# One fused diffusion block: rotation factors held per token block, and the group norm of a quarter of the tokens inside the scan's last window

## The chip, the cores and the metric

The kernel runs on one core of a Trainium2 chip. A core has TensorE (PE; its weight loads are shown apart as PEld), VectorE (DVE), ScalarE (ACT), GpSimd (POOL), and SyncE (SP), which here issues all transfers; each engine takes its own queue in order. The metric is device microseconds of one launch, the median of three runs. All arithmetic is fp32: a matmul operand is split into a high and a low part, and each product is three matmuls (high x high, low x high, high x low).

## The reference

One layer over 2048 latent tokens of width 1024 and 256 context tokens:

```
h  = modulate(rmsnorm(x)); q, k, v, rw, gl = split(h @ w_in)
q, k = apply_rope(q), apply_rope(k)                  # x*cos + swapped(x)*sin
ya = latent_window_attention(q, k, v, kc, vc, sink)  # |i-j| <= 128, and the context
y  = wkv7_scan(forward) + wkv7_scan(reverse)         # RWKV-7, 8 heads of 64
yn = (y - mu) * rsqrt(var + eps)                     # group norm, per token and head
yr = (yn * lnx_w + lnx_b + bonus) * (sigmoid(hg) @ gate_g2)
x  = x + gate1 * ((ga*(ya @ w_branch_attn) + gr*(yr @ w_branch_rwkv)) @ w_out)
x  = x + gate2 * (relu(modulate(rmsnorm(x)) @ w_up)**2 @ w_down)
```

## The kernel before

**Stages.** Projection and preparation (0 to about 1085 us) go through the tokens in blocks of up to 512 and, for each block, through groups of 128 columns of `w_in`. Each of the five groups that are rotated (four of q, one of k) calls `rope()` (L239): it loads the factors `cs` (cosine and sine, 128 x 2 x n) into the one buffer that `cs` has, copies the swapped quarters of the PSUM tile to `sw` on ACT (L245), multiplies by the sine on POOL (L246) and by the cosine on DVE (L247), and adds on POOL (L248).

The scan (about 1085 to 2401 us) has 36 steps in 9 windows of four; each step advances both directions by 64 tokens, and its chain of small matmuls (`ch`, L535, with `g` copied to SBUF by ACT at L687) is serial from step to step. Beside the chain run two generators, a piece at a time: `attend()` (attention) and `fill()` (first the merge gates, then `branch()`, L970: `ya @ w_branch_attn`, PSUM tile `gt`, results to `ma_d`). Also one piece of `ada2` (the later modulation rows, `mods`) runs per step. The first half of the steps writes y to `y_d`; the second half loads what the other direction left (`yo`), adds and stores.

The merge (about 2401 to 2797 us) takes token blocks of 512 in the order 1, 0, 2, 3. `rwkv_out(tb)` (L1141) loads `yT` from `y_d`, transposes it (`mt`, L1149), takes mean and variance per head on DVE, the power on POOL (L1160), scales on POOL (L1161), transposes back (L1170), applies `lnx_w` and `lnx_b` on ACT, adds the bonus `btile` on POOL (L1175), multiplies by the gate (matmul L1177, DVE L1178) and splits into `yr_h`, `yr_l`. Then come the `mb` matmuls (branch R, L1240 to L1242), the sum with `ma_d`, the `mm` matmuls with `w_out` (L1258 to L1260), the residual and `second_norm`. For the first block, `merge_weights()` (L1202) is called after the `mb` matmuls: it multiplies `w_out` by `gate1` (DVE L1223, tile `x1t`) and splits it into `wo_h`, `wo_l` (L1224, L1225), for use by all four blocks. The MLP (to the end) reads the second norm's output back from `h2_d` into `h2h`, `h2l`, with `up_h`, `up_l` for its first matmuls `fu`.

**What sets the order.** The program is written in one order; a scheduler then interleaves the instructions on each engine by its own simulated timeline, and the resulting order is fixed at build time. SBUF addresses come from pools, opened and closed as stacks; a tile that overlaps an earlier pool's tile waits until the last reader of that one is done.

## Time and profile before

| | |
|---|---|
| time, median of 3 runs | 4223.32 us (4220.43 to 4228.75) |
| the profiled execution | 4228.56 us, span 4226.8 us, mean granted clock 0.932 |
| PE busy | 3865.3 us, 91% |
| DVE, ACT, POOL busy | 2171.9, 1359.5, 1349.6 us |
| HBM traffic | 529.95 MB, 125 GB/s over the span |

Busy time is a sum over stages with different limits. In the MLP PE has no gap; ahead of it the gaps differ by stage. The granted clock is a share of full speed (1.0 is 2.4 GHz, 0.5 is 1.2 GHz), so a stretch at 0.5 counts as busy and still does half the work.

### The profile page before, as it was taken

Reading aid. Unit: us, or ns where it says so; the run is one execution under the profiler, and the core shown is the slowest. Engines: PE = TensorE matmul, PEld = TensorE weight load, DVE = VectorE, ACT = ScalarE, POOL = GpSimd, SP = SyncE. Lnnn points to the kernel's source line nnn. Section 1 sums busy time; section 2 is a strip of 40 time slices with the busy share of each in tenths; the row PEclk is TensorE's granted clock in tenths of the full one; section 3 lists DMA queues with packets and bytes.
Section 4 is the critical chain, followed back from the end, with each engine's and each line's share of the span. In section 5 each row is a group of like instructions: output and inputs, shape, how many; then the busy total and the mean of one; then the engine's idle time right before and its main releaser. Section 6 shows DMA issues by size and latency. Waiting matters only on the chain.

```text
span 4226.8 us, 67796 instructions
## 1 busy us (share of the span) xinstructions
PE 3865.3 (91%) x26788; PEld 3148.4 (74%) x26788; DVE 2171.9 (51%) x3794; ACT 1359.5 (32%) x2476; POOL 1349.6 (32%) x1104
## 2 busy tenths in 40 slices
PE   7989978897899989888898779989999999999999
PEld 5778868785677767766676658768888888888887
DVE  3355277767576366556566364444443345444334
ACT  2353444554343333322322233331212213112121
POOL 3353555554221110000000174533433334443231
PEclk8999979897999989797897889999999999999999
DMA  6665566666544445343442545542211214211111
GB/s 236 202 195 158 161 183 188 188 185 184 164 138 138 125 131 148 106 132 96 131 139 83 158 150 179 176 154 65 70 50 40 60 41 130 69 60 60 40 55 45
DMA packets 617587, 529.95 MB, mean 125 GB/s; under 512 B 156212, under 2 KB 536340, under 8 KB 616244
## 3 DMA queue, kind: packets, MB, share of 16 engines
q1 hardware_dynamic: 617268, 525.60, 41.6%
q8 instruction: 211, 3.46, 0.3%
q14 instruction: 108, 0.88, 0.1%
HBM read 381.09 MB, written 144.38 MB: 124 GB/s over the span
## 4 chain that ended last, share of the span: by engine, by line
PE 58%; DVE 6%; DMA 4%; issue 2%; POOL 2%; SPq 1%; ACT 1%; POOLq 0%; DVEq 0%; ACTq 0%
PE fd L1343 5%; PE fd L1344 5%; PE fd L1345 5%; PE fu L235 5%; PE fu L236 5%; PE fu L237 5%; PE ch L535 5%; PE gt L947 3%; PE ops L883 3%; PE gb L535 2%; DVE au L582 1%; PE sc L835 1%; PE mm L1260 1%; PE mm L1258 1%; PE mm L1259 1%
## 5 line engine op out<-in xcount | busy, mean ns | idle before, releaser
L235 PE MATMUL acc<-hh,w_hi 128*128 128x384 f32 (+6 forms) x1304 | 457.4, 353 | 41.6 <-ACT hh L211 18.9
L237 PE MATMUL acc<-hh,w_lo 128*128 128x384 f32 (+6 forms) x1304 | 455.8, 351 | 10.3 <-POOL w_lo L229 10.3
L236 PE MATMUL acc<-hl,w_hi 128*128 128x384 f32 (+6 forms) x1304 | 456.5, 351 | 4.8 <-POOL hl L212 4.8
L1349 DVE TENSOR_TENSOR acc<-fd,acc 128x512 f32<-128x512 f32 x480 | 322.3, 686 | 249.1 <-PE fd L1345 246.8
L235 PE MATMUL fu<-h2h,up_h 128*128 128x512 f32 x1024 | 403.4, 394 | 5.8 <-ACT rl L1330 5.8
L1343 PE MATMUL fd<-dn_h,g_h 128*128 128x512 f32 x1024 | 399.8, 390 | 3.5 <-DVE acc L1347 3.5
L236 PE MATMUL fu<-h2l,up_h 128*128 128x512 f32 x1024 | 402.6, 393 | 0.0
L237 PE MATMUL fu<-h2h,up_l 128*128 128x512 f32 x1024 | 402.0, 393 | 0.0
L1333 DVE TENSOR_TENSOR g_l<-rl,g_h 128x512 fp32r<-128x512 f32 x128 | 150.0, 1173 | 487.4 <-POOL rl L1332 487.4
L1344 PE MATMUL fd<-dn_l,g_h 128*128 128x512 f32 x1024 | 399.7, 390 | 0.0
L1345 PE MATMUL fd<-dn_h,g_l 128*128 128x512 f32 x1024 | 398.3, 390 | 0.0
L235 PEld LDWEIGHTS acc<-hh,w_hi 128*128 128x128 f32 (+2 forms) x1304 | 256.1, 197 | 67.1 <-ACT hh L211 21.8
L1332 POOL TENSOR_TENSOR rl<-rl 128x512 f32<-128x512 f32 x128 | 149.9, 1171 | 469.2 <-ACT g_h L1331 469.1
L229 POOL TENSOR_TENSOR w_lo<-w_raw,w_hi 128x1024 fp32r<-128x1024 f32 (+1 forms) x92 | 232.7, 2532 | 205.9 <-ACT w_hi L228 185.7
L1330 ACT ACTIVATE rl<-fu 128x512 f32<-128x512 f32 x128 | 76.2, 597 | 654.1 <-PE fu L237 644.9
L237 PEld LDWEIGHTS acc<-hh,w_lo 128*128 128x128 f32 (+2 forms) x1304 | 255.7, 196 | 31.4 <-POOL w_lo L229 12.5
L236 PEld LDWEIGHTS acc<-hl,w_hi 128*128 128x128 f32 (+2 forms) x1304 | 256.0, 196 | 25.1 <-POOL hl L212 6.0
L1287 POOL TENSOR_TENSOR dn_l<-raw,dn_h 128x1024 fp32r<-128x1024 f32 x64 | 155.6, 2450 | 275.1 <-ACT dn_h L1286 275.1
L845 DVE TENSOR_REDUCE mm<-sc 128x1 f32<-128x256 f32 (+1 forms) x256 | 119.0, 477 | 237.9 <-PE sc L837 152.2
L235 PEld LDWEIGHTS fu<-h2h,up_h 128*128 128x128 f32 x1024 | 193.1, 189 | 49.3 <-ACT rl L1330 6.0
L1343 PEld LDWEIGHTS fd<-dn_h,g_h 128*128 128x128 f32 x1024 | 192.9, 188 | 44.9 <-DVE acc L1347 4.0
L237 PEld LDWEIGHTS fu<-h2h,up_l 128*128 128x128 f32 x1024 | 192.7, 188 | 43.5
(305 smaller groups left out, 8292.3 us busy)
## 6 DMA issues: line engine op xcount, KB each, us to landing
w_raw<-in_w_in SPq DMA_DIRECT2D x74, 512.0 KB
raw<-in_w_mlp_up SPq DMA_DIRECT2D x64, 512.0 KB
raw<-in_w_mlp_down SPq DMA_DIRECT2D x64, 512.0 KB
bk_d<-bk SPq DMA_DIRECT2D x36, 512.0 KB
w<-v_d SPq DMA_DIRECT2D x144, 128.0 KB
gw_raw<-in_w_in SPq DMA_DIRECT2D x32, 512.0 KB
ada_w<-in_w_ada SPq DMA_DIRECT2D x32, 512.0 KB
gt<-g_d SPq DMA_DIRECT2D x64, 256.0 KB
```

The lines of the kernel that those rows point to most:

```text
L229: pool.tensor_tensor(out=lo[:, :, :m], in0=raw[:, :, :m], in1=hi[:, :, :m].bitcast(F32), op=ALU.subtract)
L235: pe.matmul(ps[:m, :n], wh[:, k, :m], hh[:, k, :], start=(k == 0), stop=False)
L236: pe.matmul(ps[:m, :n], wh[:, k, :m], hl[:, k, :], start=False, stop=False)
L237: pe.matmul(ps[:m, :n], wl[:, k, :m], hh[:, k, :], start=False, stop=(k == KC - 1))
L535: return self.link(nc.tensor.matmul(*a, **k))
L1287: eng.tensor_tensor(out=lo, in0=raw, in1=hi.bitcast(F32), op=ALU.subtract)
L1332: pool.tensor_tensor(out=rl, in0=rl, in1=rl, op=ALU.mult)
L1333: dve.tensor_tensor(out=glo[:, j], in0=rl, in1=gh[:, j].bitcast(F32), op=ALU.subtract)
L1343: pe.matmul(ps, lh, dn[j][0][:, cs], start=(j == 0), stop=False)
L1344: pe.matmul(ps, lh, dn[j][1][:, cs], start=False, stop=False)
L1345: pe.matmul(ps, ll, dn[j][0][:, cs], start=False, stop=(j == FG - 1))
L1349: dve.tensor_tensor(out=acc[:, cs], in0=ps, in1=acc[:, cs], op=ALU.add)
```

## The change

Four things. `rope()` keeps its factor tile for all groups of one token block and pass, so that 25 loads become 5; `sw` has one buffer where it had two, and `sg` of the preparation shares the buffer of `ksq`. A new generator `early()` does the whole of `rwkv_out` but the split for tokens 512 to 1023 inside the scan's last window, in four iterations of 128 tokens, with attention's PSUM banks and the SBUF buffers of four tags of the scan's pool; it stores to `yw_d`, and `rwkv_out(1)` becomes four loads and splits. The `ada2` pieces run one and two per step in turn, so that they end by step 24. `merge_weights()` is called ahead of the block loop, its gate2 part after the loop over `w_out`, and `wo_h`, `wo_l` become one tile per 128 rows, half of them in a new pool `mv` that is opened last, while `mp` (the tiles of `rwkv_out`) is opened first.

```diff
+    EB0, EBN = 512, 512
+    yw_d = dram.tile([NP, P, EBN], F32, name="yw_d")
...
+    rope_of = {}
+
     def rope(ps, t0, n, dst):
         l0 = t0 - CTX
-        cs = epool.tile([P, 2, 512], F32, name="cs", bufs=1)
-        sp.dma_start(out=cs[:, :, :n], in_=io["rope"][:, :, l0:l0 + n])
-        sw = epool.tile([P, 512], F32, name="sw")
+        if t0 not in rope_of:
+            m = 512 if n > 384 or n == 256 else 384
+            rope_of[t0] = epool.tile([P, 2, m], F32, name=f"cs{m}", bufs=1)
+            sp.dma_start(out=rope_of[t0][:, :, :n], in_=io["rope"][:, :, l0:l0 + n])
+        cs = rope_of[t0]
+        sw = epool.tile([P, 512], F32, name="sw", bufs=1)
...
-            sg = prep.tile([96, W], F32, name="sg")
+            sg = prep.tile([96, W], F32, name="sg", tag="ksq", bufs=1)
...
+    def early():
+        wk = [ip.tile([P, 4, NP, P], F32, name="yw0", tag="ga", bufs=1), ip.tile([P, 4, NP, P], F32, name="yw1", tag="st")]
+        aw = ip.tile([P, 1024], F32, name="g2e", tag="au", bufs=1)
+        sg = ip.tile([P, 2, P], F32, name="sge", tag="itmp", bufs=1)
+        g2 = aw[0:96, 0:512]
+        sp.dma_start(out=g2, in_=io["gate_g2"])
+        def load(i):
+            t0 = EB0 + i * P
+            for j in range(P // C):
+                sp.dma_start(out=wk[i % 2][:, 0, :, j * C:(j + 1) * C], in_=y_d[t0 // C + j])
+            sp.dma_start(out=sg[0:96, i % 2], in_=sg_d[:, t0:t0 + P])
+            sp.dma_start(out=wk[i % 2][:, 3], in_=bon_d[:, :, t0:t0 + P].rearrange("a p t -> p a t"))
+        load(0)
+        for i in range(EBN // P):
+            yT, yc, yw, bt = (wk[i % 2][:, j] for j in range(4))
+            s1 = aw[:, 512 + i % 2 * 2 * H:512 + (i % 2 + 1) * 2 * H].rearrange("p (b h) -> p b h", h=H)
+            if i + 1 < EBN // P:
+                load(i + 1)
+            ps = bank(atp, "ey", "at")
+            for p in range(NP):
+                pe.transpose(ps[:, p * P:(p + 1) * P], yT[:, p], ident)
+            y3 = ps.rearrange("p (h c) -> p h c", c=C)
+            dve.tensor_reduce(out=s1[:, 0], in_=y3, axis=AX.X, op=ALU.add)
+            dve.tensor_scalar(out=s1[:, 0], in0=s1[:, 0], scalar1=-1.0 / C, scalar2=None, op0=ALU.mult)
+            ycf = yc.rearrange("p a b -> p (a b)")
+            y3c = ycf.rearrange("p (h c) -> p h c", c=C)
+            dve.tensor_tensor(out=y3c, in0=y3, in1=s1[:, 0].unsqueeze(2).broadcast_to([P, H, C]), op=ALU.add)
+            act.activation(yw, yc, AF.Square)
+            dve.tensor_reduce(out=s1[:, 1], in_=yw.rearrange("p a b -> p (a b)").rearrange("p (h c) -> p h c", c=C),
+                              axis=AX.X, op=ALU.add)
+            pool.tensor_scalar(out=s1[:, 1], in0=s1[:, 1], scalar1=1.0 / C, scalar2=1e-5 * C, op0=ALU.mult, op1=ALU.add)
+            pool.tensor_tensor(out=s1[:, 1], in0=s1[:, 1], in1=expo[:, :H], op=ALU.pow)
+            pool.tensor_tensor(out=y3c, in0=y3c, in1=s1[:, 1].unsqueeze(2).broadcast_to([P, H, C]), op=ALU.mult)
+            yield
+            ps = bank(atp, "eb", "at")
+            for p in range(NP):
+                pe.transpose(ps[:, p * P:(p + 1) * P], yc[:, p], ident)
+            for p in range(NP):
+                act.activation(yw[:, p], ps[:, p * P:(p + 1) * P], AF.Identity, scale=col(O_LW + p), bias=col(O_LB + p))
+            pool.tensor_tensor(out=yw, in0=yw, in1=bt, op=ALU.add)
+            yield
+            gp = bank(atp, "eg", "at")
+            for p in range(NP):
+                pe.matmul(gp[:, p * P:(p + 1) * P], g2[:, p * P:(p + 1) * P], sg[0:96, i % 2], start=True, stop=True)
+            dve.tensor_tensor(out=yw, in0=gp.rearrange("p (a t) -> p a t", a=NP), in1=yw, op=ALU.mult)
+            sp.dma_start(out=yw_d[:, :, i * P:(i + 1) * P].rearrange("a p t -> p a t"), in_=yw)
+            yield
...
-                    next(mods, None)
+                    for _ in range(1 + step % 2):
+                        next(mods, None)
...
+                if w == NWIN - 1:
+                    ey = ey or early()
+                    for _ in range(2 - part % 2):
+                        next(ey, None)
...
-    for _ in att:
-        pass
-    for _ in flr:
-        pass
+    for it in (ey, att, flr):
+        for _ in it:
+            pass
...
+    mp = p3.enter_context(tc.tile_pool(name="mp", bufs=2, reuse_waits="tile"))
     mo = p3.enter_context(tc.tile_pool(name="mo", bufs=1, reuse_waits="tile"))
     mw = p3.enter_context(tc.tile_pool(name="mw", bufs=1, reuse_waits="tile"))
     mb = p3.enter_context(tc.tile_pool(name="mb", bufs=2, reuse_waits="tile"))
-    mp = p3.enter_context(tc.tile_pool(name="mp", bufs=2, reuse_waits="tile"))
+    mv = p3.enter_context(tc.tile_pool(name="mv", bufs=1, reuse_waits="tile"))
...
+        if EB0 <= t0 < EB0 + EBN:
+            yh = mp.tile([P, NP, TB], F32R, name="yr_h", bufs=1)
+            yl = mp.tile([P, NP, TB], F32R, name="yr_l", bufs=1)
+            for p in range(NP):
+                yw = mp.tile([P, TB], F32, name="yw")
+                sp.dma_start(out=yw, in_=yw_d[p, :, t0 - EB0:t0 - EB0 + TB])
+                split(yh[:, p], yl[:, p], yw)
+            return yh, yl
...
-    wo_h = mo.tile([P, KC, D], F32R, name="wo_h")
-    wo_l = mo.tile([P, KC, D], F32R, name="wo_l")
+    wo_h = [(mv if k < KC // 2 else mo).tile([P, D], F32R, name=f"wo_h{k}") for k in range(KC)]
+    wo_l = [(mv if k < KC // 2 else mo).tile([P, D], F32R, name=f"wo_l{k}") for k in range(KC)]
...
+        along(0, 0.5, gate1)
...
+        along(3, 1.0, (gate2[:, 0:512], gate2[:, 512:D]))
 
     blocks = (1, 0, 2, 3)
     br = rwkv_out(blocks[0])
+    merge_weights()
...
-        if at == 0:
-            merge_weights()
```

**The order on the engines.** On PE, in the last step but one before (`ch_23882` and `ch_23893` are the chain's PSUM tiles of its two directions):

```order
L535 MATMUL ch_23882<-w,bt 64x64 x8
L535 MATMUL ch_23893<-w,bt 64x64 x8
L535 MATMUL ch_23882<-bm,w 64x64 x8
L988 MATMUL gt<-ya_h,wa_h 128x512
L535 MATMUL ch_23893<-bm,w 64x64 x8
L535 MATMUL ch_23882<-kr,w 64x64 x8
L535 MATMUL ch_23893<-kr,w 64x64 x5
L989 MATMUL gt<-ya_l,wa_h 128x512
L990 MATMUL gt<-ya_h,wa_l 128x512
L988 MATMUL gt<-ya_h,wa_h 128x512
L535 MATMUL ch_23893<-kr,w 64x64 x3
L538 MATMUL tb<-ident,bks 128x128 x8
```

and in the first step of the last window after the change (`ch_23415` and `ch_23426` are the chain's tiles there; `ey`, `eb`, `eg` are the new generator's PSUM tiles):

```order
L544 MATMUL ch_23426<-w,bt 64x64 x8
L544 MATMUL ch_23415<-bm,w 64x64 x8
L544 MATMUL ch_23426<-bm,w 64x64 x8
L544 MATMUL ch_23415<-kr,w 64x64 x8
L544 MATMUL ch_23426<-kr,w 64x64
L1091 MATMUL eb<-ident,yw_23437 128x128 x4
L1098 MATMUL eg<-sge,g2e 128x128 x4
L544 MATMUL ch_23426<-kr,w 64x64 x7
L547 MATMUL tb<-ident,bks 128x128 x8
L882 MATMUL sT<-qA,kAc 128x512
L884 MATMUL sT<-qB_9589,kBc 128x512
L544 MATMUL gb<-kr,bks 128x128 x8
```

The branch matmuls (L988 to L990) that stood between the chain's are gone from there; all 96 of the last token block now stand together behind the scan. In their place stand the new transposes, `eb` among them, which reads a tile that POOL has just scaled, and attention (`sT`).

On SP, at the end of the scan, before (`y_d` is the scan's output in HBM; `ma_d` and `g_d` belong to the branch):

```order
L735 DMA y_d<-ysb 128x256
L733 DMA yo<-y_d 128x256
L983 DMA gt<-g_d 128x512
L735 DMA y_d<-ysb 128x256
L992 DMA ma_d<-gt 128x512
L1144 DMA yT<-y_d 128x4x64 x3
L983 DMA gt<-g_d 128x512
L1144 DMA yT<-y_d 128x4x64 x2
L992 DMA ma_d<-gt 128x512
L1144 DMA yT<-y_d 128x4x64 x3
L1164 DMA sgt<-sg_d 96x512
L1174 DMA btile<-bon_d 128x512 x2
```

and after:

```order
L1214 DMA yw<-yw_d 128x512 x2
L986 DMA raw<-ya_d 128x512 x2
L1192 DMA g_24431<-in_gate_g 96x512
L1314 DMA gt<-ma_d 128x512
L744 DMA y_d<-ysb 128x256
L742 DMA yo<-y_d 128x256
L1315 DMA gt<-g_d 128x512
L1214 DMA yw<-yw_d 128x512
L1202 DMA br_raw<-in_w_branch_rwkv 128x4x128
L1214 DMA yw<-yw_d 128x512
L1314 DMA gt<-ma_d 128x512
L1297 DMA x1t<-in_w_out 128x1024
```

The first block's loads are now four `yw` from `yw_d`, not eight `yT` behind the last store of `y_d`; the branch's `ya_d` loads (before, ahead of the rows shown) stand later, and the first loads of `w_out` stand in front of the branch's second half (before, all eight stood behind the `yT` loads).

On SP, at the end of the merge, before:

```order
L1197 DMA h_d<-h2f 128x512
L1283 DMA raw<-in_w_mlp_up 128x8x128 x2
L1262 DMA x_d<-x1t 128x1024
L1283 DMA raw<-h_d 128x1024 x4
L1283 DMA raw<-in_w_mlp_up 128x8x128
L1262 DMA x_d<-x1t 128x1024
L1283 DMA raw<-in_w_mlp_up 128x8x128
L1197 DMA h_d<-h2f 128x512
L1283 DMA raw<-h_d 128x1024
L1252 DMA x1t<-in_x 128x1024
```

and after:

```order
L1339 DMA x_d<-x1t 128x1024
L1272 DMA h_d<-h2f 128x512
L1329 DMA x1t<-in_x 128x1024
L1360 DMA raw<-in_w_mlp_up 128x8x128 x2
L1272 DMA h_d<-h2f 128x512
L1437 DMA gfb<-in_gf 128x1024
L1339 DMA x_d<-x1t 128x1024
L1360 DMA raw<-h_d 128x1024
L1272 DMA h_d<-h2f 128x512
L1360 DMA raw<-h_d 128x1024
```

Before, six loads of the MLP (`raw`) stood ahead of the last block's `x1t<-in_x`; after, the last block's loads of `in_x` stand first. The MLP's first tiles (`h2h`, `h2l`, `up_h`, `up_l`, `raw`) overlapped the tiles of pool `mp` before; after the change they lie where `mv` holds half of `wo_h` and `wo_l`, which the last `mm` reads.

## Rows read from the trace of the kernel before

**Rows 1.** The page: span, busy time by engine, GB/s in 40 slices.

```profile
span 4226.8 us, 67796 instructions
PE 3865.3 (91%) x26788; PEld 3148.4 (74%) x26788; DVE 2171.9 (51%) x3794; ACT 1359.5 (32%) x2476; POOL 1349.6 (32%) x1104
...
GB/s 236 202 195 158 161 183 188 188 185 184 164 138 138 125 131 148 106 132 96 131 139 83 158 150 179 176 154 65 70 50 40 60 41 130 69 60 60 40 55 45
```

**Rows 2.** Busy us by engine in 100-us stretches and the MLP.

```profile
core 0: us, PE busy (x) PEld busy (x) DVE busy (x) ACT busy (x) POOL busy (x), PEclk, DMA share, GB/s
2400.00:2500.00 100.00, 68.13 (x278) 46.28 (x273) 59.66 (x90) 25.17 (x38) 62.73 (x52) 0.80 0.57 167
...
3000.00:4200.00 1200.00, 1200.00 (x5254) 986.22 (x5253) 507.85 (x624) 258.66 (x352) 423.49 (x248) 1.00 0.19 60
```

**Rows 3.** The same columns: last scan window, scan to first `mb`, then to 2515.

```profile
2294.90:2391.40 96.50, 86.72 (x1190) 67.67 (x1192) 33.32 (x86) 27.80 (x57) 5.00 (x4) 0.92 0.40 117
2391.40:2438.70 47.30, 30.13 (x188) 20.79 (x188) 14.25 (x27) 7.87 (x14) 17.97 (x18) 0.79 0.62 177
2438.70:2515.00 76.30, 58.99 (x219) 39.83 (x218) 55.89 (x74) 26.16 (x37) 57.34 (x41) 0.79 0.57 171
```

**Rows 4.** What PE waited for, 2400 to 2530: us, times, longest.

```profile
PE mt L1170 <- DVE yc L1155: 7.7, 2, 5.3
PE gt L988 <- DVE gt L991: 6.9, 3, 5.7
PE mt L1170 <- POOL yc L1161: 6.0, 4, 2.3
PE mm L1258 <- ACT wo_h L1224: 4.1, 4, 1.9
```

**Rows 5.** Timeline of all engines: start, us, instruction, [idle before <-releaser].

```profile
2391.44 0.38 ACT L687 ACTIVATE g<-ch 128x256 f32<-128x256 f32 x1 [0.60 <-PE ch L535]
...
2409.37 0.42 DVE L734 TENSOR_TENSOR ysb<-ch,yo 128x256 f32<-128x256 f32 x1 [7.38 <-DMA yo<-y_d]
...
2410.79 1.93 SPq L1144 DMA_DIRECT2D yT<-y_d  x3
...
2415.64 0.60 PE L1149 MATMUL mt<-ident,yT 128*128 128x128 f32 x4
...
2419.82 1.66 POOL L1160 TENSOR_TENSOR s<-s,expo 128x8 f32<-128x8 f32 x1
...
2421.56 1.04 POOL L1161 TENSOR_TENSOR yc<-yc,s 128x512 f32<-128x512 f32 x1
...
2434.17 1.26 POOL L1175 TENSOR_TENSOR yw<-yw,btile 128x512 f32<-128x512 f32 x1 [1.42 <-ACT yw L1172]
...
2438.70 1.04 PE L1240 MATMUL mb<-yr_h,br_hi 128*128 128x512 f32 x2
```

**Rows 6.** Groups of instructions by line, 2438.7 to 2515: busy, mean ns, idle before.

```profile
L1223 DVE TENSOR_TENSOR x1t<-x1t,gate 128x512 f32<-128x512 f32 x16 | 21.1, 1361 | 2.0 <-DMA x1t<-in_w_out 2.0
```

**Rows 7.** The tile `cs`: instructions, what they waited for, who waited.

```profile
L242 SPq DMA_DIRECT2D cs<-in_rope x25: 550/551/3010, 33.2 to 833.6; - x25
...
  DMA cs<-in_rope: 57.0, 19
...
  PE acc L235: 12.2, 4
```

**Rows 8.** Busy us, as Rows 2, in two stretches with rotation.

```profile
420.00:490.00 70.00, 67.19 (x343) 60.40 (x341) 15.30 (x24) 39.62 (x71) 41.94 (x28) 1.00 0.57 159
780.00:850.00 70.00, 55.24 (x295) 51.64 (x294) 55.68 (x97) 37.85 (x85) 40.04 (x46) 0.80 0.72 207
```

**Rows 9.** Start of the MLP: busy as Rows 2, timeline as Rows 5.

```profile
2797.40:2860.00 62.60, 50.08 (x201) 39.70 (x200) 31.16 (x34) 22.51 (x33) 25.96 (x15) 0.86 0.39 126
...
2815.52 1.06 ACT L1286 ACTIVATE h2h<-raw 128x1024 fp32r<-128x1024 f32 x1 [1.89 <-DMA raw<-h_d]
...
2820.13 0.79 PE L235 MATMUL fu<-h2h,up_h 128*128 128x512 f32 x1 [5.79 <-ACT rl L1330]
```

More of the change, by code (lines that the diff above doesn't have):

```diff
@@ L1055, in beside @@
             credit -= 1
+    ey = None
     mods = (x for m in range(4) for x in ada2(m))
@@ L1206, in merge_weights, with along @@
         gate1 = [mw.tile([P, 512], F32, name="gate1", tag="wt", bufs=2) for hf in range(2)]
-        for m, half, dst in ((0, 0.5, gate1), (3, 1.0, (gate2[:, 0:512], gate2[:, 512:D]))):
+        def along(m, half, dst):
             for hf in range(2):
@@ L1223, in merge_weights @@
                 dve.tensor_tensor(out=raw[:, cs], in0=raw[:, cs], in1=gate1[hf], op=ALU.mult)
-            act.activation(wo_h[:, k], raw, AF.Copy)
-            (pool, dve)[k % 2].tensor_tensor(out=wo_l[:, k], in0=raw, in1=wo_h[:, k].bitcast(F32), op=ALU.subtract)
+            act.activation(wo_h[k], raw, AF.Copy)
+            (pool, dve)[k % 2].tensor_tensor(out=wo_l[k], in0=raw, in1=wo_h[k].bitcast(F32), op=ALU.subtract)
+        along(3, 1.0, (gate2[:, 0:512], gate2[:, 512:D]))
     blocks = (1, 0, 2, 3)
     br = rwkv_out(blocks[0])
+    merge_weights()
     for at, tb in enumerate(blocks):
@@ L1257, in tile_hybrid_block @@
                     lh, ll = mh[:, k, i * P:(i + 1) * P], ml[:, k, i * P:(i + 1) * P]
-                    pe.matmul(ps, lh, wo_h[:, k, cs], start=(k == 0), stop=False)
-                    pe.matmul(ps, lh, wo_l[:, k, cs], start=False, stop=False)
-                    pe.matmul(ps, ll, wo_h[:, k, cs], start=False, stop=(k == KC - 1))
+                    pe.matmul(ps, lh, wo_h[k][:, cs], start=(k == 0), stop=False)
+                    pe.matmul(ps, lh, wo_l[k][:, cs], start=False, stop=False)
+                    pe.matmul(ps, ll, wo_h[k][:, cs], start=False, stop=(k == KC - 1))
                 dve.tensor_tensor(out=x[:, cs], in0=ps, in1=x[:, cs], op=ALU.add)
```

## The prediction

> **What bounds the kernel now.** I read the page first: PE is busy for 91% of the span and no other engine for more than 51% [rows 1]. That makes PE the engine to follow, but the share is a mean over stages. The stretches say where PE still loses time. In the MLP it loses none: 5254 matmuls fill 1200 us at full clock, 0.228 us each, and only work that is taken from PE could shorten it [rows 2]. Between 2400 and 2500 us PE is busy for 68.13 of 100 us, at a mean granted clock of 0.80 [rows 2]; this is where the scan ends and the merge begins. Cut at its events it has two parts. From `g` of the last scan step (2391.44) to the first `mb` matmul (2438.70) pass 47.3 us, and from there to 2515 another 76.3 us [rows 3, 5]. Busy time multiplied by the clock is roughly work at full speed: 30.13 x 0.79 = 23.8 us in the first part and 58.99 x 0.79 = 46.6 us in the second. So 23.5 and 29.7 us are lost there, 53 us together. The list of PE's waits names their causes: `rwkv_out`'s tile `yc` (from DVE and from POOL), the branch's `gt`, the weights `wo_h` [rows 4]. The timeline shows why `yc` is late. `yT` can only be loaded (2410.79) after the last y is added and stored (DVE at 2409.37), its transposes start at 2415.64, and POOL ends the scaling at 2421.56 + 1.04 = 2422.60: 7.0 us of mean, variance, power and scaling while PE has little else [rows 5]. In the second part DVE is busy for 55.89 and POOL for 57.34 of 76.3 us [rows 3], and the largest single group on DVE is the preparation of `w_out`, 21.1 us for 16 multiplications, 1.36 us each [rows 6]: block 0's group norm, the `gt` sums and the weights all fall together there.
>
> **The transition, the main term.** The change takes block 1's group norm out of the first part, since `rwkv_out(1)` becomes four loads and splits, and moves the preparation of `w_out` forward from the second. What stands in front of the first `mb` then is the branch: before, most of its matmuls stood between the chain's; now all 96 of the last block stand together behind it. They are 96 x 0.228 = 21.9 us of PE, and they need `ya_d` to be stored by attention, loaded and split; a load of this kind takes some 5 us (2410.79 to 2415.64 [rows 5]), and SP has `yw` loads ahead of it. I put the first branch matmul 15 us after the last `g` (between 5 and 20), so that `mb` starts after 15 + 21.9 + 3 = 40 us, against 47.3. In the second part the 46.6 us of work remain. The preparation of `w_out` now runs beside the branch, where DVE was busy for 14.25 and POOL for 17.97 of 47.3 us [rows 3]; DVE's load in the second part falls by 21.1 us to 35, and POOL's, the larger, to some 50 since its quarter of the splits goes too. With a loss of 12 us where there were 29.7 it takes 59. Together 99 for 123.6: **25 us less**. Transfers set a floor: 177 GB/s for 47.3 us and 171 GB/s for 76.3 us are 8.4 + 13.0 = 21.4 MB, which at 236 GB/s, the highest slice of the page [rows 1, 3], take 91 us, so that the gain can't much exceed 33. The other bound: if the first part stays at 47.3, because the loads of `w_out` crowd those of `ya_d`, and the second keeps two thirds of its loss, 10 us remain.
>
> **The early group norm.** Each of its four iterations puts 12 narrow matmuls on PE, at 0.60 / 4 = 0.15 us [rows 5]: 1.8 us, 7.2 in all. PE's work in the last window was 86.72 x 0.92 = 79.8 of 96.5 us [rows 3], and the branch's matmuls leave it, so this has room. POOL was busy there for 5.00 us and DVE for 33.32 of 96.5. What can cost is order: PE takes its queue in turn, and `eb` stands in it ahead of chain matmuls, yet can't run until DVE, ACT and POOL have ended the 7.0 us of the same work as before [rows 5]. Between `ey` and `eb` the order holds most of a step's chain, some 10 of the step's 24 us, so most of that is covered: I take 1 us for each iteration, **4 us**. Below: nothing. Above, with no cover at all: 4 x 7.0 = 28 us. A page speaks against this part: by the Trainium skill, "SBUF — State Buffer", section Who interferes with whom, a DVE instruction with two SBUF inputs and a GpSimd instruction that reads SBUF shut each other out for the whole instruction. By it the scan's DVE work would wait at worst for POOL's power, scaling and sum, 4 x (1.66 + 1.04 + 1.26) = 16 us [rows 5], and at DVE's 35% share of that window for about 5; by the sum's own row, idle time on both engines, it would be nothing. The sum keeps the 4.
>
> **The pieces of `ada2`** that no longer run in the last 12 steps give the last window about 4 x 8 matmuls at 86.72 / 1190 = 0.073 us [rows 3], 2.3 us, and take as much from steps ahead of it. The chain's waits cover both; I cost them at nothing, with 2 us either way.
>
> **The start of the MLP.** Before, its first loads stood ahead of the last block's, into memory that `rwkv_out` had left, and its `fu` matmuls mixed with the last `mm`. Even so the start was lossy: from the last `mm` (2797.4) to 2860 stand 201 matmuls, 45.9 us of work in 62.6, 16.7 us lost, 5.8 of it in one wait [rows 9]. After the change these tiles lie where the last `mm` still reads `wo_h` and `wo_l`, so nothing can be fetched ahead. Then two loads of `up` and four of `h_d`, 512 KB each, 3.1 MB, must come in: 13.3 us at 236 GB/s [rows 1], plus the last split, 1.06 us on ACT [rows 9] and about as much on DVE, plus about 3 us at the lower clock after the gap (the clock was 0.86 over this stretch before [rows 9]). That is 18.5 us, and the later waits of the start stay in part: 16.7 becomes about 22, **5 us more**. Bounds: nothing, and 16.7 more when the old losses come on top unchanged.
>
> **The rotation.** The trace has 25 loads of `cs`, and DVE and POOL idled 57.0 us for them in 19 places [rows 7]. But where PE is the engine that counts, this is hidden: from 420 to 490 us several rotations wait for their factors one after another, and PE is busy for 67.19 of 70 us at full clock [rows 8]. PE itself waited for the rotation for 12.2 us in 4 places [rows 7], mostly between 780 and 850, where DVE is busy for 55.68 of 70 us and PE for 55.24 at 0.80 [rows 8]; DVE is late there for its own load as much as for `cs`. I take a third of the 12.2: **4 us less**. Bounds: all 12 less; and 9 more, three further stalls of 12.2 / 4 = 3 us, since `sw` with one buffer makes ACT's copies wait for POOL, and `sg` now waits for the use of `ksq`.
>
> **The sum.** -25 + 4 + 5 - 4 = -20 us. The profiled execution's 4228.56 becomes 4208.6; it lay 5.2 us above the median of the three runs, so the forecast for the median is **4203 us**. A measurement can tell about 0.2% from no change, 8.4 us.
>
> **The rivals.** (a) *Slower: the early norm holds up the chain.* If each iteration's path (7.0 us to `eb`, then ACT, POOL's sum of 1.26 and two more pieces of 0.6 on PE, about 9.5) goes into the serial chain in full, the last window grows by 38 us, and 4203 - 4 + 38 = 4237. For it: PE's order holds `eb` and `eg` in front of chain matmuls, and POOL's chain alone is 1.66 + 1.04. Against it: the distance from `ey` to `eb`. It decides from 6 us for each iteration: then nothing of the 20 and the 4 is left. By the Trainium skill's page "SBUF — State Buffer" the lock would add to it, 4203 + 5 = 4208 by the mean and 4215 at worst. (b) *The hole is one of transfers.* If the second part's losses are SP's and the DMA engines', at 171 GB/s already [rows 3], the work moved forward meets them there and only 10 of the 25 us come: 4218, which can't be told from no change. For it: `yT`, `gt` and `w_out` share one queue. Against it: 21.4 MB take 91 us at a rate that the kernel does reach. (c) *The MLP's start costs all of 16.7:* 4203 + 12 = 4215, no change that can be told. (d) *The rotation gives all of its 12 and the transition its 33:* 4203 - 8 - 8 = 4187.
>
> **How the numbers follow.** The forecast's own case (4192 to 4214) has 0.54, (d) or a part of it 0.14, (b) 0.12, (c) 0.08, (a) 0.12. The range takes in (d) and its neighbours below, (b) and (c) above, and of (a) the smaller part: 4180 to 4230 leaves out less than 2 in 10. Faster by over 0.2% (below 4214.9) are the forecast's case, (d), and a little of (b) and (c): 0.72. Within 0.2%: the rest of (b) and (c) and the mild form of (a), 0.16. Slower (above 4231.8): the full form of (a), 0.12.
>
> **What would show it.** In the profile of the changed kernel: the time from the last `g` to the first `mb` about 40 us, and PE's waits for `yc` and `wo_h` ahead of block 1's `mm` gone; the last four steps together at 96.5 to 104 us; no `fu` before the last `mm`, and then one gap of 13 to 19 us; no wait for `cs` except the first of each block, and PE's wait for the rotation below 12.2 us. Wrong would be: chain steps of 30 us with PE waiting for POOL's `yc`; a first branch matmul later than 20 us after the last `g`; or a second part that is still 70 us long, with the DMA queue as what ends its waits.

## The result, and the profile after

The changed kernel takes 4162.75 us (median of 4 runs, 4157.87 to 4169.19) beside 4222.88 for the kernel before on the same chip: a ratio of 0.9852, 95% interval 0.9836 to 0.9867. That is 60 us faster, where 20 were forecast, and below the range. The head of the page of the profile after (answers to [rows 1]):

```profile
span 4161.9 us, 67781 instructions
PE 3825.1 (92%) x26753; PEld 3127.4 (75%) x26812; DVE 2178.4 (52%) x3794; ACT 1360.0 (33%) x2488; POOL 1332.4 (32%) x1104
```

The span is 64.9 us shorter and PE's busy time 40.2 us, with the same work: part of the saving is the same matmuls at a better clock. To see where the time came from, I cut both profiles at four events: the first and the last `g` of the scan, the first `mb` and the last `mm` of the merge. All kernels of this study are in one table, in us (each line one profiled execution; the median and the ratio are those of the timed runs against the kernel before on the same chip, which had 4220.6 to 4225.6 there).

| kernel | median | ratio, interval | to first g | scan | to first mb | to last mm | to the end |
|---|---|---|---|---|---|---|---|
| before | 4222.88 | | 1126.0 | 1265.5 | 47.3 | 358.4 | 1429.7 |
| changed | 4162.75 | 0.9852 (0.9836 to 0.9867) | 1093.0 | 1237.4 | 60.8 | 332.3 | 1438.5 |
| rope_only | 4198.26 | 0.9941 (0.9919 to 0.9963) | 1095.3 | 1273.8 | 45.6 | 354.6 | 1428.2 |
| small_bufs | 4204.35 | 0.9961 (0.9947 to 0.9975) | 1108.0 | 1264.0 | 44.6 | 358.9 | 1428.3 |
| sw_one | 4207.87 | 0.9963 (0.9947 to 0.9979) | 1112.3 | 1247.8 | 45.4 | 358.7 | 1428.0 |
| sg_ksq | 4234.32 | 1.0023 (1.0008 to 1.0039) | 1129.7 | 1286.9 | 44.9 | 358.3 | 1428.3 |
| reload | 4204.72 | 0.9949 (0.9927 to 0.9971) | 1102.8 | 1276.9 | 44.6 | 356.1 | 1427.9 |
| no_rope | 4196.85 | 0.9940 (0.9924 to 0.9955) | 1128.2 | 1243.8 | 54.9 | 331.7 | 1437.6 |
| mods_only | 4199.87 | 0.9951 (0.9936 to 0.9965) | 1133.0 | 1238.5 | 40.3 | 358.1 | 1428.3 |
| mods_two | 4220.86 | 0.9982 (0.9968 to 0.9995) | 1121.3 | 1257.5 | 42.4 | 360.5 | 1427.1 |
| no_ada_load | 4165.07 | 0.9867 (0.9838 to 0.9897) | 1125.2 | 1208.9 | 45.4 | 359.1 | 1427.4 |
| ada_unread | 4196.02 | 0.9926 (0.9904 to 0.9948) | 1124.4 | 1225.1 | 44.8 | 356.5 | 1427.5 |
| ada_to_dram | 4244.12 | 1.0064 (1.0044 to 1.0084) | 1182.1 | 1230.9 | 44.8 | 357.3 | 1427.4 |
| mods_gw | 4201.11 | 0.9958 (0.9943 to 0.9973) | 1090.3 | 1280.2 | 59.6 | 333.1 | 1437.7 |
| no_early | 4176.40 | 0.9896 (0.9870 to 0.9923) | 1093.3 | 1251.8 | 36.6 | 352.5 | 1438.6 |
| pool_old | 4182.70 | 0.9905 (0.9878 to 0.9932) | 1093.7 | 1244.3 | 49.1 | 366.2 | 1427.0 |
| fw_mb | 4141.83 | 0.9828 (0.9804 to 0.9852) | 1092.5 | 1238.9 | 68.2 | 335.2 | 1399.8 |
| fw_mods2 | 4148.54 | 0.9817 (0.9800 to 0.9833) | 1099.7 | 1255.4 | 61.9 | 338.9 | 1400.0 |

Of the 64.9 us between the first two lines, 33.0 are won before the scan starts and 28.1 in the scan. The merge and the MLP together, on which the prediction spent most of its words, give 3.8. The stretches of the changed kernel that answer to [rows 3] (last scan window, last `g` to first `mb`, the 76.3 us after it) and to the window of [rows 9] (from the last `mm`):

```profile
core 0: us, PE busy (x) PEld busy (x) DVE busy (x) ACT busy (x) POOL busy (x), PEclk, DMA share, GB/s
2241.70:2330.30 88.60, 80.71 (x1150) 66.83 (x1156) 39.44 (x95) 32.70 (x72) 16.84 (x17) 0.90 0.43 118
2330.30:2391.10 60.80, 40.00 (x208) 28.60 (x209) 24.79 (x31) 12.22 (x20) 18.10 (x12) 0.78 0.74 220
2391.10:2467.40 76.30, 69.87 (x307) 54.99 (x306) 45.61 (x65) 24.79 (x40) 46.38 (x38) 0.96 0.54 168
2723.80:2786.40 62.60, 44.81 (x184) 35.29 (x183) 29.05 (x31) 26.85 (x37) 27.57 (x15) 0.81 0.57 178
```

The last window is 8 us shorter though POOL now has 16.84 us of work in it. The stretch to the first `mb` is 13.5 us longer. The 76.3 us behind it hold 307 matmuls where there were 219, at clock 0.96 for 0.79: of the 29.7 us that were lost there, 76.3 - 69.87 x 0.96 = 9.2 are left. The MLP's start does 184 matmuls where there were 201.

PE's waits from the last `g` on (answers to [rows 4]) and two stretches of the hole that is left:

```profile
PE gt L997 <- DVE gt L1000: 10.8, 7, 3.4
PE gt L997 <- ACT ya_h L987: 3.7, 2, 3.0
...
PE gt L998 <- POOL ya_l L988: 3.2, 2, 2.3
```

```profile
2340.00:2350.00 10.00, 5.19 (x14) 3.36 (x13) 4.38 (x7) 4.09 (x6) 7.25 (x6) 0.67 0.98 324
2350.00:2360.00 10.00, 5.27 (x12) 3.42 (x12) 5.01 (x4) 1.58 (x2) 4.43 (x3) 0.50 1.18 270
```

The waits for `yc` and `wo_h` are gone. The branch waits instead. PE stands for 20.8 of the 60.8 us to the first `mb`, and the waits for `gt` make up the larger part: 10.8 us for DVE, since the PSUM tile has one bank and after each group of 12 matmuls PE stands until DVE has read it, and 6.9 for the splits `ya_h` and `ya_l` of what attention stored. With the gaps the granted clock falls to 0.50, the lower of its two levels, from 2350 to 2360. DVE's rows there (start, us, instruction):

```profile
2355.58 0.68 DVE L1000 SCALAR_TENSOR_TENSOR gt<-gt 128x512 f32<-128x512 f32 x1
2361.84 0.69 DVE L1000 SCALAR_TENSOR_TENSOR gt<-gt 128x512 f32<-128x512 f32 x1 [5.58 <-PE gt L999]
...
2366.06 2.29 DVE L1302 TENSOR_TENSOR wo_l<-x1t,wo_h 128x1024 fp32r<-128x1024 f32 x1 [1.13 <-ACT wo_h L1301]
2368.27 0.67 DVE L1000 SCALAR_TENSOR_TENSOR gt<-gt 128x512 f32<-128x512 f32 x1
```

From one of DVE's sums to the next a group takes 6.3 us at the lower clock (2355.58 to 2361.84), instead of the 2.7 of its matmuls at full clock. The next one takes 6.4 us though its matmuls ran at full clock (from 2362.58, 0.24 us from start to start): DVE was preparing `wo_l`, which the change had moved beside the branch, and PE stood 3.40 us for it. The last ones take 3.8 us (2383.73, 2387.53).

### The profile page after: what moved, and what is told of

Its sections match the earlier page's. It is cut to its first block, busy times and chain, and to the rows that moved or that the text cites. A ratio compares the mean times of both kernels' runs of the same rounds, so it can differ in the third digit from the quotient of the medians.

```text
span 4161.9 us, 67781 instructions
## 1 busy us (share of the span) xinstructions
PE 3825.1 (92%) x26753; PEld 3127.4 (75%) x26812; DVE 2178.4 (52%) x3794; ACT 1360.0 (33%) x2488; POOL 1332.4 (32%) x1104
## 4 chain that ended last, share of the span: by engine, by line
PE 58%; DVE 7%; DMA 5%; issue 2%; POOL 2%; ACT 2%; SPq 1%; another core or an unknown queue 1%; POOLq 0%; ACTq 0%; DVEq 0%
PE fu L238 6%; PE fu L239 6%; PE fu L240 6%; PE fd L1421 6%; PE fd L1420 6%; PE fd L1422 6%; PE ch L544 5%; PE ops L892 3%; PE gt L956 3%; PE gb L544 2%; DVE au L591 1%; PE mm L1335 1%; PE mm L1336 1%; PE mm L1337 1%; PE sc L844 1%
## 5 line engine op out<-in xcount | busy, mean ns | idle before, releaser
L1410 DVE TENSOR_TENSOR g_l<-rl,g_h 128x512 fp32r<-128x512 f32 x128 | 158.8, 1241 | 476.2 <-POOL rl L1409 476.0
L232 POOL TENSOR_TENSOR w_lo<-w_raw,w_hi 128x1024 fp32r<-128x1024 f32 (+1 forms) x92 | 224.2, 2439 | 219.1 <-ACT w_hi L231 202.1
L1407 ACT ACTIVATE rl<-fu 128x512 f32<-128x512 f32 x128 | 76.3, 597 | 653.4 <-PE fu L240 648.5
L239 PEld LDWEIGHTS fu<-h2l,up_h 128*128 128x128 f32 x1024 | 192.9, 188 | 43.5 <-DVE h2l L1364 0.8
```

The costliest lines, as they stand in the source:

```text
L232: pool.tensor_tensor(out=lo[:, :, :m], in0=raw[:, :, :m], in1=hi[:, :, :m].bitcast(F32), op=ALU.subtract)
L239: pe.matmul(ps[:m, :n], wh[:, k, :m], hl[:, k, :], start=False, stop=False)
L1410: dve.tensor_tensor(out=glo[:, j], in0=rl, in1=gh[:, j].bitcast(F32), op=ALU.subtract)
```

## The experiments

**Which part gives what.** Four kernels, each with one part alone or left out.

`rope_only` is the kernel before with the change's `rope()` and its line on `sg`; `no_rope` is the changed kernel with both as before. The other two:

```diff
@@ mods_only, on the kernel before
-                    next(mods, None)
+                    for _ in range(1 + step % 2):
+                        next(mods, None)
@@ no_early, on the changed kernel
-                if w == NWIN - 1:
-                    ey = ey or early()
-                    for _ in range(2 - part % 2):
-                        next(ey, None)
...
-        if EB0 <= t0 < EB0 + EBN:
...
```

> The kernel before with the first part alone: factors held per token block, one sw buffer, sg in ksq's buffer. Theory 1, the rotation is what shortens the projection by some 33 us (on SP a load of cs waits for the last group's readers, and the loads behind it in the queue wait with it): 4190 us, with the scan's first g at about 1093 us instead of 1126. Rival, the rotation was hidden as the prediction had it and the projection's gain is the reordering that comes with the other parts: 4215 to 4220 us, first g at 1120 or later.

> The kernel before with the pieces of ada2 one and two per step in turn, nothing else. Theory 2, the scan's gain of some 28 us between its first and last g comes from these pieces leaving the last steps: 4195 to 4205 us, with the projection unchanged. Rival, it comes from the early norm and the branch that moves out of the steps: 4218 to 4227 us.

> The changed kernel with the old rotation (25 loads, two sw buffers, sg with its own buffer). Theory 1: 4163 + 31 = 4194 us. Rival, the rotation was hidden: 4163 to 4170 us.

> The changed kernel without the early group norm: block 1 goes through the whole of rwkv_out after the scan, as before; rotation, ada2 pieces, pools and the earlier merge_weights stay. If the early norm and the branch's move give the scan's last window and the transition what they gain (some 20 + 8 us): 4190 us. If the early norm only moves the time from the scan to the branch: 4163 to 4170 us, with a longer last window and a shorter time from the last g to the first mb than the 60.8 us of the changed kernel.

Theories 1 and 2 held. The rotation alone gives 0.59% (25 us), and taking it out of the changed kernel loses 0.88% (37 us); in the profiles with the old `rope()` and `sw` the scan starts at 1121 to 1133 us (but for `ada_to_dram`, below), in those with the new ones at 1090 to 1100. The `ada2` pieces alone give 0.49% (21 us), all of it in the scan. The two parts by themselves give 46 of the 60 us, if their gains add up, which isn't shown: the rotation is worth 25 us alone and 37 in the changed kernel. Without the early norm the changed kernel is 0.44% slower (19 us), against an expected 27 or none; of this 14.4 us lie in the scan, and the way from the last `g` to the last `mm` is even 4 us shorter without it (389.1 for 393.1). The last window, the time to the first `mb` and the 76.3 us behind it, without the early norm:

```profile
2242.60:2345.10 102.50, 89.45 (x1152) 70.69 (x1154) 31.57 (x80) 28.59 (x58) 7.81 (x7) 0.86 0.42 126
2345.10:2381.70 36.60, 21.84 (x165) 14.75 (x164) 12.36 (x24) 6.61 (x12) 15.26 (x15) 0.74 0.51 140
2381.70:2458.00 76.30, 59.53 (x239) 42.80 (x238) 61.16 (x76) 23.64 (x34) 52.55 (x35) 0.88 0.56 174
```

The last window is 13.9 us longer and holds 60 branch matmuls (13.7 us at 0.228) where the changed kernel has none. Behind it the first part is 24.2 us shorter and the second does 68 matmuls fewer. So the early norm pays in the scan, not behind it: there it only moves the loss from the second part to the first.

**What it is in the rotation.** Four more kernels on the kernel before.

```diff
@@ small_bufs: both; sw_one: the first; sg_ksq: the second
-        sw = epool.tile([P, 512], F32, name="sw")
+        sw = epool.tile([P, 512], F32, name="sw", bufs=1)
-            sg = prep.tile([96, W], F32, name="sg")
+            sg = prep.tile([96, W], F32, name="sg", tag="ksq", bufs=1)
@@ reload, on small_bufs
+        m = 512 if n > 384 or n == 256 else 384
-        cs = epool.tile([P, 2, 512], F32, name="cs", bufs=1)
+        cs = epool.tile([P, 2, m], F32, name=f"cs{m}", bufs=1)
```

> The kernel before with one sw buffer and sg in ksq's buffer, the 25 loads of cs into one buffer as before. If holding the factors is what shortens the projection: no gain here, 4221 to 4230 us, first g at 1126 or later. Rival, the other layout and the reordering that comes with it shorten it: 4195 to 4205 us, first g near 1095.

> As the run before, but cs gets two tiles by the block's size (512 and 384) as in the change, and is still loaded 25 times. Neighbouring groups of a pass use the two in turn, so that a load does not wait for the group just ahead. If the wait for the single buffer is the cost: about all of the rotation's gain, 4195 to 4203 us. If the 20 transfers and their place in SP's queue are the cost: little of it, 4213 to 4222 us.

> The kernel before with one sw buffer alone (sg keeps its own). If this is what gave 17 us to the kernel with both small edits: 4200 to 4208 us, first g near 1108. If sg in ksq's buffer gave it: 4216 to 4226 us, first g at 1125 to 1133 as in all profiles with the old rotation.

> The kernel before with sg in ksq's buffer alone. The single sw buffer alone gave 13 of the 17 us of both; so 4217 to 4224 us and first g at 1120 to 1130. If any small edit that changes the order in the projection wins as much: 4200 to 4210.

Theory 1 fell in its strong form: with 25 loads into one buffer, and only the two small edits, 16 of the 25 us are there, and the single `sw` buffer alone gives as much (0.9963), while `sg` alone costs some 10 where a gain of a few had been expected. What a second buffer for `cs` and then the holding add can't be told by the times, whose intervals overlap; the projection's end shows them, 1108.0, 1102.8, 1095.3. Counting `acc` matmuls along the projection, the five profiled so with one `sw` buffer (`rope_only`, `small_bufs`, `sw_one`, `reload` and the changed kernel) win 14 to 16 us between 250 and 373 us, right behind the first block's rotations. Of this the last 4 to 5 us, from 350 on, aren't the buffer's: four kernels with the old rotation win them too. SP's rows there, of the kernel before (start, us, what is issued), and the wait of PE that hangs on them:

```profile
244.68 1.76 SPq L242 DMA_DIRECT2D cs<-in_rope  x1
246.53 1.02 SPq L204 DMA_DIRECT2D hf<-h_d  x2
...
253.94 0.80 SPq L204 DMA_DIRECT2D hf<-h_d  x2
257.81 0.32 SPq L407 DMA_DIRECT2D v_d<-vt  x1
...
260.50 4.65 SPq L204 DMA_DIRECT2D hf<-h_d  x1
...
268.19 1.22 PE L235 MATMUL acc<-hh,w_hi 128*128 128x512 f32 x2 [6.19 <-ACT hh L211]
```

and with one `sw` buffer:

```profile
243.03 3.02 SPq L204 DMA_DIRECT2D hf<-h_d  x2
246.15 0.66 SPq L242 DMA_DIRECT2D cs<-in_rope  x1
251.02 0.33 SPq L204 DMA_DIRECT2D hf<-h_d  x1
...
251.91 4.81 SPq L204 DMA_DIRECT2D hf<-h_d  x2
256.81 0.38 SPq L407 DMA_DIRECT2D v_d<-vt  x1
```

With one buffer the scheduler puts the loads of the next block's activations (`hf`) ahead of the load of `cs` and of the stores of `v_d`; before, they stood behind those stores, for which SP waited 3.0 us on ACT, one of them was issued only by 260.50 + 4.65 = 265.15, and PE stood 6.19 us for it. That wait is 1.0 us in the second kernel. It is about half of the 10 to 11 us won up to 350; the other half wasn't traced, and no run changes the order on SP alone. In the changed kernel the rotation no longer waits for the load of `cs`; what DVE and POOL wait for there is ACT's copies (answers to [rows 7]), and PE waits 1.9 us for the rotation, in one place:

```profile
L250 SPq DMA_DIRECT2D cs<-in_rope x5: 586/614/888, 34.2 to 467.2; - x5
...
  ACT sw L254: 75.8, 26
...
  PE acc L238: 1.9, 1
```

**What it is in the `ada2` pieces.** Each piece loads 512 KB of `w_ada` into the buffer that attention uses for its query (`tag="qraw"`, one buffer), multiplies, and adds on DVE. Five kernels.

```diff
@@ no_ada_load, on the kernel before (ada_unread keeps the two first lines, and its matmuls read silr)
-            wt = ap_.tile([P, D], F32, name="ada_w2", tag="qraw", bufs=1)
-            sp.dma_start(out=wt, in_=w_ada[:, k, (2 + m) * D:(3 + m) * D])
+            wt = silr.rearrange("p a b c -> p (a b c)")
@@ ada_to_dram, on no_ada_load
+            sp.dma_start(out=ada_d[m * KC + k], in_=w_ada[:, k, (2 + m) * D:(3 + m) * D])
@@ mods_two, on the kernel before
-                    next(mods, None)
+                    for _ in range(2):
+                        next(mods, None)
@@ mods_gw, on the changed kernel, with four pieces per step
-            wt = ap_.tile([P, D], F32, name="ada_w2", tag="qraw", bufs=1)
+            wt = gap.tile([P, KC, P], F32, name="ada_w2", tag="gw_raw").rearrange("p a b -> p (a b)")
```

> The kernel before with its ada2 pieces one per step as before, all matmuls and sums kept, but without the 32 loads of w_ada in the scan: the matmuls read a tile that is there (so the modulation of the second half is another, and its time alone counts). If the pieces cost because their load shares one buffer and the queue with attention's query load: the scan from first to last g falls by the 27 us of the kernel with the pieces moved or more, 1230 to 1240 us, and the time to 4185 to 4198. If their matmuls and sums cost: 1260 us or more and 4215 to 4225.

> The kernel before with its ada2 loads at their places and in the query's buffer, one per step, but nothing reads them: the matmuls read a tile that is there (another modulation, the time alone counts). If the shared buffer and SP's queue are the cost: scan 1250 to 1265 us and 4210 to 4222, with ACT and DVE still waiting some 50 us for the query. If PE and DVE waiting in order for the load are: 1205 to 1225 us and 4163 to 4185, as without the loads.

> As the run without the loads of w_ada in the scan (same matmuls on a tile that is there, so another modulation), but the 32 transfers are issued again at their places, 512 KB each, to a scratch in HBM: SP's queue and the transfers are back, the buffer shared with attention's query load is not. If the shared buffer is the cost: scan from first to last g 1205 to 1220 us, time 4163 to 4176. If the transfers or SP's time are: 1240 to 1265 us, 4195 to 4221.

> The kernel before with two ada2 pieces in each step, so that they end by step 18. If a piece costs only in the late steps: scan 1230 to 1240 us, as with one and two in turn, or 5 less; 4190 to 4200. If each piece costs the same wherever it stands, and the gain with one and two in turn was one of order: 1250 to 1265 us, 4210 to 4222.

> The changed kernel with the ada2 pieces four per step and their load in the buffer of the gate weights' raw tile instead of the query's; they end with the gates, early in the scan. If sharing with the query load still costs the changed kernel some 28 of the 57 us: scan 1205 to 1220 us instead of 1237, 4135 to 4150 us. If the gates now wait for these loads instead: 4163 to 4180 us.

Without the loads the scan is 56.6 us shorter, with all matmuls and sums in place: the loads are the cost, and twice what the change recovers in the scan. With the loads in place and nobody reading them, 1225.1 us: about 40 of the 57 in the profile, and 31 us by the ratio, between the two theories. What was waited for at the tile `qraw` (us, times), kernel before:

```profile
  ACT qA L812: 33.9, 12
  DMA qraw<-q_d: 23.9, 10
...
  PE sc L835: 11.9, 3
```

without the loads, and with loads that nobody reads:

```profile
  ACT qA L812: 5.7, 5
  DMA qraw<-q_d: 0.9, 1
```

```profile
  ACT qA L812: 13.3, 8
  DMA qraw<-q_d: 0.8, 1
```

DVE's and ACT's waits for the query fall from 57.8 to 6.6 and 14.1 us. So the load holds the query's buffer until PE has read it, and attention starts each block later; when nobody reads, the buffer is free as soon as the load lands. What this leaves of the cost for the readers' own waits was not separated, and a buffer of its own for the load was not tried. `ada_to_dram` doesn't tell the buffer from the queue: without a buffer to wait for, all 32 transfers went out between 30.3 and 76.4 us and delayed the projection by 56 us. But its scan, too, is one without these loads and with the same matmuls, and it takes 1230.9 us, 22.0 more than that of `no_ada_load`. So the order alone moves the scan by some 20 us from kernel to kernel, and the loads cost 35 to 57 us of it.

Two pieces per step give only 0.18%, so the gain does not follow from how early the pieces end. By windows of four steps, `mods_two` takes 24 us more than the kernel before in steps 0 to 11 and 32 less behind them; `mods_only` takes the same in steps 0 to 15 and 26 less behind them. So a piece isn't free in the early steps. With the pieces in the gate weights' buffer and four per step (`mods_gw`) the scan is 43 us longer than in the changed kernel, and the time lies 21 us above the slower of the two ranges that I had given; since pace and buffer change together there, it doesn't show what sharing with that load costs.

With one and two pieces in turn the scan gains 10.5, 8.6 and 10.0 us in steps 20 to 23, 24 to 27 and 28 to 31; the last piece runs at 2002 us, at the end of step 23. The kernel before, in two stretches of late steps, and `mods_only` over the same work:

```profile
1925.00:2110.00 185.00, 151.56 (x1849) 118.03 (x1847) 116.09 (x260) 53.76 (x103) 7.50 (x8) 0.81 0.39 111
...
2245.00:2295.00 50.00, 37.70 (x401) 29.47 (x399) 29.25 (x59) 10.52 (x19) 0.00 (x0) 0.64 0.25 72
```

```profile
1930.00:2095.00 165.00, 142.67 (x1849) 112.86 (x1847) 116.87 (x260) 53.79 (x103) 7.55 (x8) 0.86 0.44 123
...
2244.00:2270.00 26.00, 23.11 (x388) 18.85 (x388) 16.76 (x32) 8.02 (x16) 0.00 (x0) 0.97 0.30 83
```

The same 1849 matmuls take 20 us less. In the kernel before, one step took 50 us in the second stretch: attention's last query load went out at 2248.0, the next `ada2` load stood in SP's queue until DVE had read it (2253.65), and the chain's loads behind it waited.

**The MLP's start.** Two other layouts of the changed kernel, and the faster one with two pieces per step.

```diff
@@ pool_old, on the changed kernel (mp is opened last, too)
-    mv = p3.enter_context(tc.tile_pool(name="mv", bufs=1, reuse_waits="tile"))
+    mv = mo
@@ fw_mb, on the changed kernel (mb is opened right behind mp, too)
+    fw = p4.enter_context(tc.tile_pool(name="fw", bufs=2, reuse_waits="tile"))
     hp = p4.enter_context(tc.tile_pool(name="h2", bufs=1, reuse_waits="tile"))
...
-    fw = p4.enter_context(tc.tile_pool(name="fw", bufs=2, reuse_waits="tile"))
@@ fw_mods2, on fw_mb
-                    for _ in range(1 + step % 2):
+                    for _ in range(2):
```

> The changed kernel with the pools of the merge as before: mp opened last, all of wo_h and wo_l in mo, no mv. The first loads of the MLP can run ahead again: from the last mm to the end 1429 us where the changed kernel has 1438.5. If the merge is no slower for it: 4153 to 4158 us. If the weights' tiles now have to wait for the scan's: the time from the last g to the last mm rises above 393 us by what is won or more, 4163 to 4175 us.

> The changed kernel with the pool of the MLP's first tiles opened first, and mb opened behind mp, so that these tiles lie over mp and mb, which are free before the last mm; in the order fu stands ahead of the last mm again. If the lost prefetch is what the MLP's start costs: last mm to end 1427 to 1430 us instead of 1438.5, all else as it was, 4151 to 4157 us. If the layout costs the merge what it gives the MLP, as with the old pools: 4163 to 4180 us.

> The changed kernel with the MLP's first tiles over mp and mb (4141.83 us) and two ada2 pieces in each step. If pieces are free in the early steps and still cost in steps 18 to 24: 4130 to 4140 us. If not: 4142 to 4155.

With the old pools the MLP takes 1427.0 us again, but the way from the last `g` to the last `mm` loses 22 us (415.3 for 393.1), more than I had expected, and the whole is slower than the changed kernel (0.9905). In `fw_mb` the MLP's first tiles lie over pools that are free before the last `mm`; `fu` starts at 2718.2, 17 us ahead of the last `mm` (2734.8), and PE has no gap at all:

```profile
2734.80:2797.40 62.60, 62.60 (x285) 51.82 (x284) 34.92 (x41) 23.71 (x36) 27.01 (x17) 1.00 0.37 121
```

From the last `mm` to the end it takes 1399.8 us, 38.7 less than the changed kernel and 29.9 less than the kernel before, much more than the 10 that I expected; the way to the last `mm` gives 10 back. Of the 38.7 us, 20.7 are the loss of the changed kernel's start, and 5 are the 21 `fu` matmuls ahead of the last `mm`. Some 11 more come from the body of the MLP:

```profile
2937.00:4050.00 1113.00, 1113.00 (x4912) 921.59 (x4911) 483.24 (x579) 246.04 (x332) 398.24 (x232) 1.00 0.20 62
```

That is 0.2266 us for a matmul, where the kernel before takes 0.2284 [rows 2], both at full clock and without a gap. Taken apart by tile, a `fu` matmul follows the one ahead of it after 0.2267 us, in the changed kernel after 0.2301; the second matmuls of the MLP (`fd`) take 0.227 in both. With 3072 `fu` matmuls this is 10.4 us. What it is in the other layout that makes `fu` faster was not traced.

At 4141.83 us (0.9828) it is the fastest median, but its interval overlaps that of the changed kernel from 0.9836 to 0.9852. With two pieces per step the ratio is 0.9817, not to be told from 0.9828, but its interval (0.9800 to 0.9833) lies below that of the changed kernel.

## Why the prediction was wrong

It forecast 4203 us, with a range from 4180, and the time is 4162.75. Step by step:

- **The pieces of `ada2`, "I cost them at nothing, with 2 us either way".** This step failed outright. It priced the matmuls (2.3 us) and left out what its own rule demanded: the transfer of a moved step, the buffer it lands in and the queue it stands in. Measured: 21 us for the move by itself, 35 to 57 for all loads.
- **The rotation, "4 us less", bounds 12 less to 9 more.** Measured 25 alone. The holding as such gives 8 to 13 us of the projection (1102.8 or 1108.0 to 1095.3), within the bounds, a size that the times don't settle. What failed is the sentence on the small edits: the single `sw` buffer was taken for a risk of 9 us and gave some 16, in part through another order on SP. A price from the waits of PE that name the rotation can't see that; the 6.19 us that went away are booked under `hh`.
- **The transition, "25 us less".** The second part did as argued: its work was prepared ahead, PE ran at 0.96, and 9.2 us were lost where 12 were forecast. The first part did not: 60.8 us instead of 40. The first branch matmul came 8.1 us after the last `g` (2338.40), earlier than the 15 of the sum. But from there to the first `mb` passed 52.7 us, because the 21.9 us for the branch were a sum of matmuls at full clock: left out were the waits for `gt`'s one bank and for the splits of `ya`, and the lower clock behind them. Before, 60 of the 96 stood behind the last `g` as well, in the same groups, but the chain's last matmuls and block 1's transposes stood between some of these. Nor was the group norm in PE's way as the prediction read it: in the 7.0 us in which PE was said to have "little else" it was busy for 5.25:

```profile
2415.64:2422.60 6.96, 5.25 (x29) 3.87 (x27) 4.99 (x9) 1.26 (x2) 2.90 (x3) 1.00 0.76 193
```

  From the last `g` to the last `mm` 12.6 us were won, and 22 `fu` matmuls (5.0 us) are no longer among them: 8 in truth. The early norm has no share in these (389.1 us without it); with the old pools (`pool_old`) they turn into a loss, so they rest on the layout, which the prediction counted only as a cost.
- **The early norm, "4 us".** The sign was wrong. The last window fell from 96.5 to 88.6 us, and is 102.5 without the early norm; PE waited once for `eb`, 0.4 us. The branch that left the steps counted, and I had noted that it leaves and given it no price. Rival (a) is refuted by the same row:

```profile
PE eb L1091 <- POOL yw L1087: 0.4, 1, 0.4
```

  As to the lock between DVE and GpSimd that the Trainium skill states ("SBUF — State Buffer", Who interferes with whom): the chain's own DVE instructions there took a mean of 421 ns (`w`, L719) beside 422 before, with three times POOL's work next to them. They read one operand from PSUM, so the rule wouldn't count them; no delay of the chain shows. The prediction's 16 and 5 us had counted all of DVE's work in the window. Of those with two tiles as operands only `qB` (twice, 684 ns before and after) and some of under 0.2 us have both in SBUF there, so this case hardly tests the rule.
- **The start of the MLP, "5 us more".** Right: 62.6 us with 184 matmuls (41.9 us of work) lose 20.7 us where 16.7 were lost, 4 more. (Before, nine of the MLP's loads stood ahead of the last block's `in_x` in the order shown above, not six.) That the whole loss could be avoided, the prediction did not see, and its sentence that in the MLP only work taken from PE could save time is refuted by `fw_mb`, where the same `fu` matmuls run faster.
- **The terms together.** The early norm, the weights and the layout were forecast at -25 + 4 + 5 = -16 us; the changed kernel less the two other parts by themselves is 0.9852 - (0.9941 + 0.9951 - 1) = -0.40%, 17 us. So the size of the main argument came out right by luck: the gain lies in the scan and not in the transition, and it holds only if the parts add up (with the 37 us that the rotation is worth in the changed kernel, 5 us would be left). The 40 us that are missing are the two parts that were costed at 4 and at nothing. The floor of 91 us for transfers was none: 236 GB/s is the mean of a slice of 106 us, and SP's transfers ran at 324 GB/s in 10 us of the hole.

What stays open: which neighbours make a piece cheap in the first 16 steps at one and two in turn and dear at two per step, where the other half of the gain of `sw` comes from, and how far single edits like it would keep their worth under another order. The ten runs of `sw_one` spread over 21 us, and one profile each can't tell stages 10 us apart in the scan.

## What to carry to other kernels

Price an edit by the resources that it holds (buffer, queue place, bank), not by its arithmetic: here 32 loads into a shared buffer cost 35 to 57 us, with all their arithmetic left in place. Where a scheduler orders one queue for all transfers, a change of a buffer count is a change of order, and its effect is found under other names in the list of waits. When work is taken out of the gaps of a serial chain and put together behind it, look for what the gaps had hidden, such as a single PSUM bank, and for what else its reader has to do there.

## What the runs showed of the hardware

The 16 DMA engines moved 324 GB/s in 10 us of the merge's start (2340 to 2350). The highest of the kernel before's 40 slices was 236 [rows 1], but a slice is a mean over 106 us; in single stretches of 10 us that kernel moves more than either:

```profile
10.00:20.00 10.00, 6.28 (x27) 0.92 (x26) 3.82 (x6) 1.59 (x4) 1.89 (x4) 1.00 1.01 424
```

In the branch, where PE worked and stood in turn, the granted clock was 0.50 for 10 us (2350 to 2360), so that a group of 12 matmuls and its wait took 6.3 us there and 3.8 us some 28 us later. And at full clock and without a gap a matmul of the MLP's first half (`fu`, 128x512) took 0.2301 us from start to start in the changed kernel and 0.2267 in `fw_mb`.
